# SBUF sums of a hybrid decoder layer: from GpSimd to VectorE, and the last norm's column sums ahead of its output products

## The chip, the cores and the metric

One core of one Trainium2 chip. The metric is the device time of one execution in microseconds (us), the median of three runs. The engines, as the profile names them: PE is TensorE (matmul), DVE is VectorE, ACT is ScalarE, POOL is GpSimd, SP is SyncE, which here issues all DMAs.

## The reference, cut to what matters

One decoder layer on 1024 tokens of width 1024, all in float32: an RMS norm and one input projection, split between dilated attention (8 heads) and an mLSTM (4 heads); an output projection; an MLP of width 4096; a gated embedding; a final norm.

```python
u = rms_norm(h, norm_mix_g); proj = u @ w_in
mix = concat([dilated_attention(q, k, v), mlstm(qc, kc, vm, i, f) * sigmoid(mo)])
h = h + mix @ w_out
u = rms_norm(h, norm_mlp_g)
h = h + square(relu(u @ w_up)) @ w_down
gate = sigmoid(rms_norm(h, norm_ple_g) @ w_ple_gate)
h = h + gate * (p @ w_ple)
return rms_norm(h, final_norm_g)
```

## The kernel before

Activations lie transposed: 128 features on the partitions, 1024 tokens along the free dimension, eight such tiles. Every float32 product is made of three fp32r matmuls (`mm3`, L101 to L103): an operand is split into a high part (ACT casts, L92) and a low part (DVE subtracts the high part, L93, or L85 in `load_w`), and high by high, high by low and low by high are summed in PSUM.

The stages, in the order of time:

- **Mixing** (to 560 us): the projections of q, k, v and the mLSTM's operands, the attention, the gates and the mLSTM heads. A tile scheduler that simulates the program chooses the order on each engine; projection matmuls stand between the attention's as filler. GpSimd does here the low parts of 24 weight tiles (`load_w(..., eng=G)`, L85), the rotation's product with the sines (`rope`, L339), two terms of the first norm's sum (L212), five sums on the gates' 32 rows (L263 to L278), the mask added to the decay rows `w` (`mlstm`, L594) and a sum of two blocks (L620).
- **Rest of the output projection and the operands** (560 to 660 us): the MLP's product is done by a scheme of seven block products in place of eight (`OPS`), so sums and differences of blocks are formed first: `operands` (L797) for the activations, `load_blocks` (L759 to L761, three sums to a weight block) for the weights, all on GpSimd.
- **Up-projection** (660 to some 970 us): 16 passes of `products`, two weight blocks each; `store` squares the result and writes it to DRAM (`zd`).
- **Down-projection** (some 970 to 1295 us): seven steps (`D_OPS`: b11, b21, t1, t2, b22, t3, t4) of eight groups `g`. Each group loads `y_r` and `wd_r` by DMA, splits both (L92, L93: `yh`/`yl`, `wdh`/`wdl`) and does 24 matmuls. Steps t1, t2, b22 and t3 need differences of weight blocks, which `weights` forms on GpSimd (L968, L975, L971). `wd_r` has four buffers, the split tiles three.
- **Gate, embedding and final norm** (1295 to 1395 us): `embed`, `gate`, then for four quarters of the output `final_cols(i)` (column sums on PE, a power on GpSimd, L1181) and `final(i)` (rows spread by PE, products on DVE, or on ACT and GpSimd, and the output's DMA). `ON_V[i]` lists the tiles whose product DVE does.

Each engine works through its own queue strictly in order, so an instruction that waits holds up all that stand behind it. GpSimd also has the powers (`pow`), and one-element copies (L1075) that make a DMA wait for a split.

Of the kernel before, what the change touches and what calls it, by code (L numbers as in the profile page):

```python
# [16 lines left out]
P = 128  # L17
# [28 lines left out]
def layer_kernel(ctx, tc, xT, wqk, wv, wvg, wmv, wmqk, wmo, wout, wup, wdown, wpg, wple, pT,  # L46
# [157 lines left out]
    for k in range(KT):  # L204
        if k:
            xr = unit("xr", F32)
            nc.sync.dma_start(xr, xT[k])
            X.append(split(pair("x"), xr, col[:, C_GMIX + k:C_GMIX + k + 1]))
        S.activation(xr, xr, AF.Square)
        eng = G if k in (1, 3) else V  # L210
        if eng in acc:
            eng.tensor_tensor(acc[eng], acc[eng], xr, op=ALU.add)  # L212
        else:
            acc[eng] = xr
        if k == 5:
            V.tensor_tensor(acc[V], acc[V], acc[G], op=ALU.add)
    col_sum(ssum, acc[V])
# [26 lines left out]
    def gates():  # L244
        g0, g1, g2, g3 = [unit("g", F32) for _ in range(4)]
        gb = col[:, C_GB:C_GB + 1]
        fr, t1, m, A, ir = g1[:R], g2[:R], g2[:R], g3[:R], g0[:R]
        wide = g3[:, :NB * 2 * R].rearrange("p (b g r) -> p b g r", b=NB, g=GC)
        S.copy(wide, gcol.unsqueeze(3).to_broadcast([P, NB, GC, NB]))
        for c in range(NCH):  # L250
            sl = slice(c * CH, (c + 1) * CH)
            ps = pmm.tile([P, CH], F32, name="g", tag="mm")
            for b in range(NB // 2):
                i = (c * NB // 2 + b) * 2 * R
                PE.transpose(ps[:2 * R, b * P:(b + 1) * P], g3[:, i:i + 2 * R], ident)
            S.activation(fr[:, sl], ps[R:2 * R], AF.Identity, bias=gb[R:2 * R])
            S.activation(ir[:, sl], ps[:R], AF.Identity, bias=gb[:R])
        V.scalar_tensor_tensor(t1, fr, -1.0, fr, op0=ALU.mult, op1=ALU.max)
        S.activation(t1, t1, AF.Exp, scale=-1.0)
        S.activation(t1, t1, AF.Ln, bias=1.0)  # L260
        V.scalar_tensor_tensor(fr, fr, 0.0, t1, op0=ALU.min, op1=ALU.subtract)
        V.tensor_tensor_scan(m, fr, ir, 0.0, op0=ALU.add, op1=ALU.max)
        G.tensor_tensor(ir, ir, m, op=ALU.subtract)  # L263
        G.tensor_tensor(fr[:, 1:], fr[:, 1:], m[:, :T - 1], op=ALU.add)
        G.tensor_tensor(fr, fr, m, op=ALU.subtract)
        mk = unit("mk", F32)[:R]
        nc.sync.dma_start(mk, maskT)
        G.tensor_tensor(fr, fr, mk, op=ALU.mult)
        V.tensor_tensor_scan(A, mk, fr, 0.0, op0=ALU.mult, op1=ALU.add)

        for j in range(T // 256):
            t0 = j * 256
            nc.sync.dma_start(arow[:, j, :256], A[2 * j::NB, t0:t0 + 256])
            nc.sync.dma_start(arow[:, j, 256:], A[2 * j + 1::NB, t0 + P:t0 + 256])
        nc.sync.dma_start(mk, lastT)
        end = sm.tile([R, 1], F32, name="end", bufs=1)
        V.tensor_tensor_reduce(mk, mk, A, 1.0, 0.0, op0=ALU.mult, op1=ALU.add, accum_out=end)
        G.tensor_tensor(ir, ir, A, op=ALU.subtract)  # L278
        return ir, m, end
# [19 lines left out]

    def values(src, evac, name, cw=256, eng=G):  # L300

# [32 lines left out]
    def rope(ps, sl):  # L334
        q = mp.tile([P, CH], F32, name="q")
        sh = mp.tile([P, CH], F32, name="sh")
        V.stream_shuffle(sh, ps, [i ^ 8 if i < 16 else i for i in range(32)])
        V.tensor_tensor(q, ps, cosS[:, sl], op=ALU.mult)
        G.tensor_tensor(sh, sh, sinS[:, sl], op=ALU.mult)  # L339
        V.tensor_tensor(q, q, sh, op=ALU.add)  # L340
        return q
# [4 lines left out]
    def project_qk(p, w=None):  # L346
# [22 lines left out]
        if w is None:  # L369
            proj(pmm, load_w(wqk[p], "wq", eng=G), X, ev_q, "q")  # L370
            proj(pmm, load_w(wqk[4 + p], "wk", eng=G), X, ev_k, "k")
            return QS, KD, kl
# [78 lines left out]
    def conv_silu(ct, stage, to=None):  # L451
# [4 lines left out]
        def ev(ps, c, sl):  # L456
# [14 lines left out]
            if to is None:  # L471
                nc.sync.dma_start(qkd[ct, :, sl], y)
        proj(pmm, load_w(wmqk[ct], "wm", eng=G), X, ev, "m")

    def out_gate(h, stage):

        def ev(ps, c, sl):
# [109 lines left out]
    def mlstm(h, c, ops, out):  # L587
# [5 lines left out]
        diag = w2.rearrange("p i (b s) -> p i b s", s=P)[:, :, 0::2]  # L593
        G.tensor_tensor(diag, diag, below.unsqueeze(1).unsqueeze(1).to_broadcast([P, 2, 2, P]), op=ALU.add)  # L594
        for i in range(2):
# [4 lines left out]
        for i in range(2):  # L600
# [15 lines left out]
            for b, at, n, t0 in blocks:  # L616
                bs = slice(b * P, (b + 1) * P)
                mm3(num[:, o + L - n:o + L], v[0][:, bs], v[1][:, bs], ph[:, at:at + n], pl[:, at:at + n],
                    j == 0 and at == 0, at > 0)
            G.tensor_tensor(w[:, P:L], w[:, P:L], w[:, L:], op=ALU.add)  # L620
            if j:
# [92 lines left out]
    with ExitStack() as tail:  # L714
# [38 lines left out]

        def load_blocks(src, name, raw=None, pool=None, eng=G):
            if raw is None:
                raw = wtc.tile([P, 8, L], F32, name=name + "_r", tag="wc", bufs=2)
            if src is not None:
                nc.sync.dma_start(raw[:, :4], src)
            eng.tensor_tensor(raw[:, 4:7:2], raw[:, 2:3].to_broadcast([P, 2, L]), raw[:, 1:4:2], op=ALU.subtract)  # L759
            eng.tensor_tensor(raw[:, 5], raw[:, 3], raw[:, 4], op=ALU.subtract)  # L760
            eng.tensor_tensor(raw[:, 7], raw[:, 0], raw[:, 5], op=ALU.subtract)  # L761
            wa = split(wtile(name, 3, "wa", pool), raw[:, 3:6])
# [25 lines left out]
        def operands(src, new, temp):  # L788
# [173 lines left out]
        def weights(key, g):  # L962
# [169 lines left out]
        def gate(k, sl, src, ga):  # L1132
# [82 lines left out]
        for o in range(1, NO - 1):  # L1215
# [92 lines left out]
```

## Time and profile before

| what | value |
|---|---|
| median of three runs | 1397.48 us (1396.22 to 1398.34) |
| the profiled execution's own time | 1397.32 us |
| its span, first to last instruction | 1395.5 us |
| PE busy | 1337.2 us, 96% of the span |
| DVE busy | 1018.9 us, 73% |
| ACT busy | 654.7 us, 47% |
| POOL busy | 408.2 us, 29% |
| mean granted TensorE clock | 0.984 of full speed |

All profile numbers come from one execution, the profiled one. An engine's busy time is the time in which one of its instructions ran; an instruction that was held up while it ran counts as busy for all of that time. Idle time of an engine that nobody waits for costs nothing.

### The profile page before, as it was taken

The numbers are of one execution on the slowest core, as the hardware profiler recorded it, in microseconds if no ns is written. First come the engines' busy times: TensorE is split into PE (matmuls) and PEld (weight loads), VectorE is DVE, ScalarE is ACT, GpSimd is POOL, SyncE is SP. The second block draws the span as 40 slices with busy tenths as digits, with TensorE's granted clock in tenths as the row PEclk, the third lists the DMA queues.
The fourth block names the chain that finished last, engine by engine and source line by source line (L and its number), as shares of the span: only waits on it lengthen the run. The fifth ranks groups of instructions, "written<-read, shape, count | busy, mean of one in ns | idle before, by whom it ended". The sixth has DMA issues, their size and how long they took to land.

```text
span 1395.5 us, 18439 instructions
## 1 busy us (share of the span) xinstructions
PE 1337.2 (96%) x6795; PEld 1121.1 (80%) x6795; DVE 1018.9 (73%) x1558; ACT 654.7 (47%) x1036; POOL 408.2 (29%) x271
## 2 busy tenths in 40 slices
PE   8999999999979999999999999999999899999995
PEld 6978988977868887787888888888887688888875
DVE  7788679589859796597566676567558965778896
ACT  6556545644446343256443334435334233465553
POOL 1432031142103222056333443332006771311012
PEclk9999999999999999999999999999999999999997
DMA  6111012222225347554164444446869674481323
GB/s 231 46 50 37 22 51 62 61 91 84 76 71 196 128 138 241 200 185 179 46 223 154 166 157 175 151 152 253 322 231 322 245 247 144 151 301 61 106 83 128
DMA packets 79017, 208.25 MB, mean 149 GB/s; under 512 B 7536, under 2 KB 19728, under 8 KB 74320
## 3 DMA queue, kind: packets, MB, share of 16 engines
q1 hardware_dynamic: 78928, 207.09, 43.1%
q8 instruction: 53, 0.87, 0.3%
q14 instruction: 36, 0.29, 0.1%
HBM read 146.74 MB, written 60.32 MB: 148 GB/s over the span
## 4 chain that ended last, share of the span: by engine, by line
PE 50%; DVE 11%; DMA 7%; issue 3%; POOL 2%; ACT 2%; SPq 0%; DVEq 0%; POOLq 0%; ACTq 0%
PE u L102 7%; PE u L103 7%; PE u L101 7%; PE d L102 6%; PE d L103 6%; PE d L101 6%; DMA wd_r<-wdown 2%; DMA w<-arow 1%; DMA wpg_r<-wpg 1%; POOL s L968 1%; DVE yl L93 1%; DMA in<-mixmd 1%; PE mo L101 1%; PE o L103 1%; PE mo L103 1%
## 5 line engine op out<-in xcount | busy, mean ns | idle before, releaser
L102 PE MATMUL u<-x,wuh 128*128 128x512 f32 x448 | 178.4, 398 | 0.2 <-DVE x L93 0.2
L101 PE MATMUL u<-x,wuh 128*128 128x512 f32 x448 | 176.0, 398 | 1.5 <-ACT x L92 1.5
L102 PE MATMUL d<-yl,wdh 128*128 128x512 f32 x432 | 169.0, 392 | 7.3 <-DVE yl L93 7.3
L103 PE MATMUL u<-x,wul 128*128 128x512 f32 x448 | 173.4, 398 | 0.0
L103 PE MATMUL d<-yh,wdl 128*128 128x512 f32 x432 | 168.3, 391 | 0.0
L101 PE MATMUL d<-yh,wdh 128*128 128x512 f32 x432 | 166.6, 391 | 0.0
L93 DVE TENSOR_TENSOR wul<-wu_r,wuh 128x768 fp32r<-128x768 f32 (+1 forms) x64 | 72.3, 1130 | 78.8 <-ACT wuh L92 78.8
L101 PEld LDWEIGHTS u<-x,wuh 128*128 128x128 f32 x448 | 84.9, 190 | 22.6 <-ACT x L92 2.4
L102 PEld LDWEIGHTS d<-yl,wdh 128*128 128x128 f32 x432 | 81.5, 189 | 25.9 <-DVE yl L93 8.9
L102 PEld LDWEIGHTS u<-x,wuh 128*128 128x128 f32 x448 | 85.0, 190 | 20.7 <-DVE x L93 0.5
L759 POOL TENSOR_TENSOR wu_r<-wu_r 128x512 f32<-128x512 f32 x32 | 47.0, 1468 | 186.3 <-DMA wu_r<-wup 161.2
L103 PEld LDWEIGHTS u<-x,wul 128*128 128x128 f32 x448 | 85.0, 190 | 20.1
L92 ACT CAST wuh<-wu_r 128x768 fp32r<-128x768 f32 (+1 forms) x64 | 60.5, 946 | 78.7 <-POOL wu_r L760 55.2
L103 PEld LDWEIGHTS d<-yh,wdl 128*128 128x128 f32 x432 | 81.6, 189 | 16.9
L101 PEld LDWEIGHTS d<-yh,wdh 128*128 128x128 f32 x432 | 81.4, 189 | 16.9
L93 DVE TENSOR_TENSOR yl<-y_r,yh 128x1024 fp32r<-128x1024 f32 x54 | 89.8, 1664 | 0.0
L93 DVE TENSOR_TENSOR wdl<-wd_r,wdh 128x1024 fp32r<-128x1024 f32 x30 | 42.5, 1416 | 51.3 <-ACT wdh L92 51.3
L412 ACT ACTIVATE pr<-pr,mn 128x128 f32<-128x128 f32 (+3 forms) x64 | 49.5, 774 | 56.0 <-PE av L415 30.4
L92 ACT CAST wdh<-wd_r 128x1024 fp32r<-128x1024 f32 x30 | 31.5, 1051 | 73.4 <-PE d L102 54.2
L92 ACT CAST wdh<-s 128x1024 fp32r<-128x1024 f32 x24 | 25.2, 1048 | 84.1 <-issue 70.5
L911 ACT COPY tmp<-u 128x512 f32<-128x512 f32 x48 | 28.0, 586 | 77.9 <-PE u L103 77.9
L93 DVE TENSOR_TENSOR wdl<-s,wdh 128x1024 fp32r<-128x1024 f32 x24 | 37.3, 1555 | 36.1 <-ACT wdh L92 36.1
(398 smaller groups left out, 3754.0 us busy)
## 6 DMA issues: line engine op xcount, KB each, us to landing
wd_r<-wdown SPq DMA_DIRECT2D x72, 512.0 KB
y_r<-zd SPq DMA_DIRECT2D x56, 512.0 KB
wu_r<-wup SPq DMA_DIRECT2D x32, 512.0 KB
zd<-zz SPq DMA_DIRECT2D x16, 1024.0 KB
zd<-zt SPq DMA_DIRECT2D x16, 1024.0 KB
wm_r<-wmqk SPq DMA_DIRECT2D x8, 512.0 KB
wo_r<-wout SPq DMA_DIRECT2D x16, 256.0 KB
hs<-h SPq DMA_DIRECT2D x8, 512.0 KB
```

Of the source, the lines that this page charges most:

```text
L92: S.copy(hi, src)
L93: V.tensor_tensor(lo, src, hi.bitcast(F32), op=ALU.subtract)
L101: PE.matmul(ps, wh, xh, start=start, stop=False, skip_group_check=more)
L102: PE.matmul(ps, wh, xl, start=False, stop=False, skip_group_check=more)
L103: PE.matmul(ps, wl, xh, start=False, stop=stop, skip_group_check=more)
L412: S.activation(pr[:, :nk], pr[:, :nk], AF.Exp, scale=-1.0, bias=mn[:, :1], accum_out=den)
L759: eng.tensor_tensor(raw[:, 4:7:2], raw[:, 2:3].to_broadcast([P, 2, L]), raw[:, 1:4:2], op=ALU.subtract)
L911: S.copy(tmp[key], ps)
L968: G.tensor_tensor(sw[g], a, b, op=ALU.subtract)
```

## The change

Every `tensor_tensor` sum, difference or product of SBUF tiles that GpSimd did goes to VectorE, but for the final products of the output and the powers. Since the scheduler simulates the program, the order on every engine is made anew. At the end, the column sums of all four quarters stand in the program ahead of the products of quarters 1 to 3, and `ON_V` gives DVE 6, 5 and 6 of the eight products of those quarters, where it had 6, 8 and 6.

```diff
-        eng = G if k in (1, 3) else V
+        eng = V
...
-        G.tensor_tensor(ir, ir, m, op=ALU.subtract)
-        G.tensor_tensor(fr[:, 1:], fr[:, 1:], m[:, :T - 1], op=ALU.add)
+        V.tensor_tensor(ir, ir, m, op=ALU.subtract)
+        V.tensor_tensor(fr[:, 1:], fr[:, 1:], m[:, :T - 1], op=ALU.add)
...
-    def values(src, evac, name, cw=256, eng=G):
+    def values(src, evac, name, cw=256, eng=V):
...
-        G.tensor_tensor(sh, sh, sinS[:, sl], op=ALU.mult)
+        V.tensor_tensor(sh, sh, sinS[:, sl], op=ALU.mult)
...
-            proj(pmm, load_w(wqk[p], "wq", eng=G), X, ev_q, "q")
+            proj(pmm, load_w(wqk[p], "wq", eng=V), X, ev_q, "q")
...
-        G.tensor_tensor(diag, diag, below.unsqueeze(1).unsqueeze(1).to_broadcast([P, 2, 2, P]), op=ALU.add)
+        V.tensor_tensor(diag, diag, below.unsqueeze(1).unsqueeze(1).to_broadcast([P, 2, 2, P]), op=ALU.add)
...
-            G.tensor_tensor(w[:, P:L], w[:, P:L], w[:, L:], op=ALU.add)
+            V.tensor_tensor(w[:, P:L], w[:, P:L], w[:, L:], op=ALU.add)
...
-        def load_blocks(src, name, raw=None, pool=None, eng=G):
+        def load_blocks(src, name, raw=None, pool=None):
...
-            eng.tensor_tensor(raw[:, 4:7:2], raw[:, 2:3].to_broadcast([P, 2, L]), raw[:, 1:4:2], op=ALU.subtract)
+            V.tensor_tensor(raw[:, 4:7:2], raw[:, 2:3].to_broadcast([P, 2, L]), raw[:, 1:4:2], op=ALU.subtract)
...
-                    G.tensor_tensor(ts[key][:, us], src[u][i0][:, s0], in1, op=o)
+                    V.tensor_tensor(ts[key][:, us], src[u][i0][:, s0], in1, op=o)
...
-                G.tensor_tensor(sw[g], a, b, op=ALU.subtract)
+                V.tensor_tensor(sw[g], a, b, op=ALU.subtract)
...
-                G.tensor_tensor(sw[g], a, sw[g], op=ALU.subtract)
+                V.tensor_tensor(sw[g], a, sw[g], op=ALU.subtract)
...
-                (G if c and k < 6 else V).tensor_tensor(fin[:, sl], fin[:, sl], ga, op=ALU.add)
+                V.tensor_tensor(fin[:, sl], fin[:, sl], ga, op=ALU.add)
...
-        ON_V = ((0, 1, 3, 4, 6), (0, 1, 3, 4, 5, 6), range(KT), (0, 2, 3, 5, 6, 7))
+        ON_V = ((0, 1, 3, 4, 6), (0, 1, 3, 4, 6, 7), (0, 1, 3, 4, 6), (0, 2, 3, 5, 6, 7))
...
-                                   "t3": [lambda: final_cols(1)], "t4": [lambda: final(1), lambda: final_cols(2)]})
-        final(2)
+                                   "t3": [lambda: final_cols(1)], "t4": [lambda: final_cols(2)]})
         final_cols(3)
-        final(3)
+        for i in range(1, 4):
+            final(i)
```

In the changed program the lines lie two further up from L263 on (four in the last loop but one place). Three places show what the new order does.

**Step t1 of the down-projection.** GpSimd before: `h<-yl` is the one-element copy, `s<-wd_r` a difference for t1, `s<-wd_r,s` one for t2.

```order
L968 TENSOR_TENSOR s<-wd_r 128x1024 x2
L1075 COPY h<-yl 1x1
L975 TENSOR_TENSOR s<-wd_r,s 128x1024 x2
L1075 COPY h<-yl 1x1
L975 TENSOR_TENSOR s<-wd_r,s 128x1024 x2
```

VectorE in the changed program, at the same place; before, its queue held there only the splits `wdl` and `yl`.

```order
L966 TENSOR_TENSOR s<-wd_r 128x1024
L93 TENSOR_TENSOR wdl<-s,wdh 128x1024
L996 TENSOR_TENSOR state<-state,sq 128x512
L93 TENSOR_TENSOR yl<-y_r,yh 128x1024
L973 TENSOR_TENSOR s<-wd_r,s 128x1024
L93 TENSOR_TENSOR wdl<-s,wdh 128x1024
L93 TENSOR_TENSOR yl<-y_r,yh 128x1024
L973 TENSOR_TENSOR s<-wd_r,s 128x1024 x3
L93 TENSOR_TENSOR wdl<-s,wdh 128x1024
```

The differences, each of which waits for its DMA, now stand between the splits that PE waits for.

**The end, VectorE before:** `out` is a final product (`bp_12113`, `bp_12140` and `bp_12165` are the spread rows of quarters 1, 2 and 3), `ra` the step between a quarter's column sums and its power, `h` and `state` the last gate and row sum.

```order
L1195 SCALAR_TENSOR_TENSOR out<-h,col,bp_12113 128x256 x6
L1137 SCALAR_TENSOR_TENSOR ga<-ga,e 128x256
L1138 SCALAR_TENSOR_TENSOR h<-ga,h 128x256
L1180 SCALAR_TENSOR_TENSOR ra_12136<-cs_12131,seps 128x2
L1138 SCALAR_TENSOR_TENSOR h<-ga,h 128x256
L1146 TENSOR_TENSOR state<-state,ga 128x256
L1195 SCALAR_TENSOR_TENSOR out<-h,col,bp_12140 128x256 x8
L1180 SCALAR_TENSOR_TENSOR ra_12161<-cs_12156,seps 128x2
L1195 SCALAR_TENSOR_TENSOR out<-h,col,bp_12165 128x256 x6
```

VectorE in the changed program (`bp_12131`, `bp_12149`, `bp_12168` for quarters 1, 2, 3):

```order
L1136 SCALAR_TENSOR_TENSOR h<-ga,h 128x256
L1144 TENSOR_TENSOR state<-state,ga 128x256
L1178 SCALAR_TENSOR_TENSOR ra_12118<-cs_12113,seps 128x2
L1193 SCALAR_TENSOR_TENSOR out<-h,col,bp_12131 128x256 x5
L1178 SCALAR_TENSOR_TENSOR ra_12127<-cs_12122,seps 128x2
L1193 SCALAR_TENSOR_TENSOR out<-h,col,bp_12131 128x256
L1193 SCALAR_TENSOR_TENSOR out<-h,col,bp_12149 128x256 x5
L1193 SCALAR_TENSOR_TENSOR out<-h,col,bp_12168 128x256 x6
```

The last gate steps come before the products of quarter 1, and the last `ra` before those of quarter 2. GpSimd's queue there is now:

```order
L1179 TENSOR_TENSOR rb_12119<-ra_12118,mhalf 128x2
L1196 TENSOR_TENSOR out<-out,rows 128x256 x5
L1179 TENSOR_TENSOR rb_12128<-ra_12127,mhalf 128x2
L1196 TENSOR_TENSOR out<-out,rows 128x256 x2
```

Before, the powers of quarters 2 and 3 followed each other; now five products of quarters 1 and 2 stand between them.

**End of the attention, PE before:** `mvp` is the last projection filler, `s`, `tp` and `av` are the attention's scores, transposes and value products.

```order
L103 MATMUL mvp<-mv_h,x 128x256
L405 MATMUL s<-kd,qs 128x512
L406 MATMUL s<-kl_120,qs 128x512
L405 MATMUL s<-kd,qs 128x256
L406 MATMUL s<-kl_120,qs 128x256
L422 MATMUL tp<-ident,pr 128x128 x3
```

PE in the changed program:

```order
L103 MATMUL mvp<-mv_h,x 128x256
L429 MATMUL av<-ph,vv 128x256
L430 MATMUL av<-pl,vv 128x256
L429 MATMUL av<-ph,vv 128x128
L430 MATMUL av<-pl,vv 128x128
L420 MATMUL tp<-ident,pr 128x128 x8
L413 MATMUL av<-ident,den 128x128 x2
```

From the last filler to the next projection matmul stand 95 matmuls before and 139 in the changed program: the filler is used up earlier.

## Rows read from the trace of the kernel before

**Rows 1.** The page, part 1: busy us (share of the span) xinstructions

```profile
PE 1337.2 (96%) x6795; PEld 1121.1 (80%) x6795; DVE 1018.9 (73%) x1558; ACT 654.7 (47%) x1036; POOL 408.2 (29%) x271
```

**Rows 2.** Stretches of 50 us: PE, PEld, DVE, ACT, POOL busy (x), PEclk, DMA share, GB/s

```profile
300.00:350.00 50.00, 48.66 (x260) 39.70 (x259) 47.70 (x94) 19.98 (x49) 12.80 (x5) 1.00 0.28 95
...
600.00:650.00 50.00, 49.54 (x213) 39.64 (x212) 45.05 (x40) 31.70 (x40) 32.64 (x19) 1.00 0.54 189
...
1050.00:1100.00 50.00, 44.19 (x191) 35.25 (x189) 46.51 (x25) 22.07 (x26) 36.97 (x17) 1.00 0.81 285
```

**Rows 3.** Waits: who waited for whom: us in total, times, longest us

```profile
PE d L102 <- DVE yl L93: 7.3, 4, 3.5
...
PE bp L130 <- POOL rb L1181: 6.8, 3, 3.2
...
POOL w L594 <- DMA w<-arow: 62.1, 6, 40.3
```

**Rows 4.** Timeline, GpSimd and VectorE, step t1: start us, us, engine line op

```profile
1079.33 4.74 POOL L975 TENSOR_TENSOR s<-wd_r,s 128x1024 f32<-128x1024 f32 x2
...
1079.25 5.90 DVE L93 TENSOR_TENSOR yl<-y_r,yh 128x1024 fp32r<-128x1024 f32 x1
```

**Rows 5.** Groups of VectorE by shape: count | busy us, mean ns | idle before

```profile
L93 DVE TENSOR_TENSOR yl<-y_r,yh 128x1024 fp32r<-128x1024 f32 x54 | 89.8, 1664 | 0.0
...
L93 DVE TENSOR_TENSOR y<-y_r,y 128x1024 fp32r<-128x1024 f32 x2 | 2.4, 1216 | 0.6 <-ACT y L92 0.6
...
L759 DVE TENSOR_TENSOR wpg_r<-wpg_r 128x512 f32<-128x512 f32 x8 | 5.5, 689 | 4.8 <-DMA wpg_r<-wpg 4.8
...
L760 DVE TENSOR_TENSOR wpg_r<-wpg_r 128x256 f32<-128x256 f32 x8 | 3.3, 417 | 0.0
...
L93 DVE TENSOR_TENSOR wdl<-wd_r,wdh 128x1024 fp32r<-128x1024 f32 x30 | 42.5, 1416 | 51.3 <-ACT wdh L92 51.3
...
L93 DVE TENSOR_TENSOR wdl<-s,wdh 128x1024 fp32r<-128x1024 f32 x24 | 37.3, 1555 | 36.1 <-ACT wdh L92 36.1
```

**Rows 6.** Five stretches about the places of the change, columns as in group 2

```profile
60.00:387.50 327.50, 318.59 (x1937) 277.89 (x1937) 261.63 (x594) 173.93 (x361) 76.78 (x37) 1.00 0.19 59
...
387.50:408.80 21.30, 15.79 (x97) 12.40 (x95) 14.64 (x42) 10.28 (x22) 0.00 (x0) 0.92 0.05 13
...
425.00:560.00 135.00, 131.19 (x785) 114.55 (x784) 106.20 (x228) 57.81 (x116) 35.61 (x33) 0.97 0.52 171
...
650.00:668.00 18.00, 16.24 (x57) 12.83 (x56) 11.32 (x14) 10.85 (x18) 9.39 (x9) 0.72 0.40 147
...
1057.00:1112.00 55.00, 47.75 (x200) 38.03 (x199) 53.66 (x29) 20.73 (x24) 40.20 (x19) 0.97 0.80 289
```

**Rows 7.** Timeline of the operands, GpSimd and ScalarE, before the up-projection

```profile
644.06 2.00 POOL L759 TENSOR_TENSOR wu_r<-wu_r 128x512 f32<-128x512 f32 x1 [5.64 <-DMA wu_r<-wup]
...
651.75 1.28 POOL L797 TENSOR_TENSOR t<-h,t 128x512 f32<-128x512 f32 x1
...
653.07 1.14 ACT L92 CAST x<-h 128x512 fp32r<-128x512 f32 x2 [2.39 <-POOL t L797]
```

**Rows 8.** Timeline of one pass of the up-projection

```profile
809.83 1.43 POOL L759 TENSOR_TENSOR wu_r<-wu_r 128x512 f32<-128x512 f32 x1 [0.27 <-DMA wu_r<-wup]
...
814.78 1.07 DVE L93 TENSOR_TENSOR wul<-wu_r,wuh 128x768 fp32r<-128x768 f32 x1 [0.35 <-ACT wuh L92]
...
823.35 0.57 ACT L913 COPY zz<-u 128x512 f32<-128x512 f32 x1
```

**Rows 9.** Timeline of the end, VectorE and GpSimd

```profile
1378.62 2.42 DVE L1195 SCALAR_TENSOR_TENSOR out<-h,col,bp 128x256 f32<-128x256 f32 x6
...
1383.98 3.22 DVE L1195 SCALAR_TENSOR_TENSOR out<-h,col,bp 128x256 f32<-128x256 f32 x8 [0.96 <-ACT rows L1189]
...
1387.12 0.15 DVE L1180 SCALAR_TENSOR_TENSOR ra<-cs,seps 128x2 f32<-128x2 f32 x1
...
1389.32 1.41 POOL L1198 TENSOR_TENSOR out<-out,rows 128x256 f32<-128x256 f32 x2 [1.28 <-ACT rows L1189]
```

More of the change, by code (lines that the diff above doesn't have):

```diff
@@ L214, in layer_kernel @@
             acc[eng] = xr
-        if k == 5:
-            V.tensor_tensor(acc[V], acc[V], acc[G], op=ALU.add)
     col_sum(ssum, acc[V])
@@ L262, in gates @@
         V.tensor_tensor_scan(m, fr, ir, 0.0, op0=ALU.add, op1=ALU.max)
-        G.tensor_tensor(ir, ir, m, op=ALU.subtract)
-        G.tensor_tensor(fr[:, 1:], fr[:, 1:], m[:, :T - 1], op=ALU.add)
-        G.tensor_tensor(fr, fr, m, op=ALU.subtract)
+        V.tensor_tensor(ir, ir, m, op=ALU.subtract)
+        V.tensor_tensor(fr[:, 1:], fr[:, 1:], m[:, :T - 1], op=ALU.add)
+        V.tensor_tensor(fr, fr, m, op=ALU.subtract)
         mk = unit("mk", F32)[:R]
         nc.sync.dma_start(mk, maskT)
-        G.tensor_tensor(fr, fr, mk, op=ALU.mult)
+        V.tensor_tensor(fr, fr, mk, op=ALU.mult)
         V.tensor_tensor_scan(A, mk, fr, 0.0, op0=ALU.mult, op1=ALU.add)
@@ L277, in gates @@
         V.tensor_tensor_reduce(mk, mk, A, 1.0, 0.0, op0=ALU.mult, op1=ALU.add, accum_out=end)
-        G.tensor_tensor(ir, ir, A, op=ALU.subtract)
+        V.tensor_tensor(ir, ir, A, op=ALU.subtract)
         return ir, m, end
@@ L369, in project_qk @@
         if w is None:
-            proj(pmm, load_w(wqk[p], "wq", eng=G), X, ev_q, "q")
-            proj(pmm, load_w(wqk[4 + p], "wk", eng=G), X, ev_k, "k")
+            proj(pmm, load_w(wqk[p], "wq", eng=V), X, ev_q, "q")
+            proj(pmm, load_w(wqk[4 + p], "wk", eng=V), X, ev_k, "k")
             return QS, KD, kl
@@ L472, in ev @@
                 nc.sync.dma_start(qkd[ct, :, sl], y)
-        proj(pmm, load_w(wmqk[ct], "wm", eng=G), X, ev, "m")
+        proj(pmm, load_w(wmqk[ct], "wm", eng=V), X, ev, "m")
     def out_gate(h, stage):
@@ L482, in ev @@
             nc.sync.dma_start(sgd[h, :, sl], sg)
-        proj(pmm, load_w(wmo[h], "wo", eng=G), X, ev, "mo")
+        proj(pmm, load_w(wmo[h], "wo", eng=V), X, ev, "mo")
     def stage(name):
@@ L758, in load_blocks @@
                 nc.sync.dma_start(raw[:, :4], src)
-            eng.tensor_tensor(raw[:, 4:7:2], raw[:, 2:3].to_broadcast([P, 2, L]), raw[:, 1:4:2], op=ALU.subtract)
-            eng.tensor_tensor(raw[:, 5], raw[:, 3], raw[:, 4], op=ALU.subtract)
-            eng.tensor_tensor(raw[:, 7], raw[:, 0], raw[:, 5], op=ALU.subtract)
+            V.tensor_tensor(raw[:, 4:7:2], raw[:, 2:3].to_broadcast([P, 2, L]), raw[:, 1:4:2], op=ALU.subtract)
+            V.tensor_tensor(raw[:, 5], raw[:, 3], raw[:, 4], op=ALU.subtract)
+            V.tensor_tensor(raw[:, 7], raw[:, 0], raw[:, 5], op=ALU.subtract)
             wa = split(wtile(name, 3, "wa", pool), raw[:, 3:6])
@@ L967, in weights @@
                 a, b = wraw(g, A21), wraw(g, A22)
-                G.tensor_tensor(sw[g], a, b, op=ALU.subtract)
+                V.tensor_tensor(sw[g], a, b, op=ALU.subtract)
             elif key == "t3":
                 a, b = wraw(g, A21), wraw(g, A11)
-                G.tensor_tensor(a, a, b, op=ALU.subtract)
+                V.tensor_tensor(a, a, b, op=ALU.subtract)
                 return a
@@ L1120, in fetch @@
                         G.tensor_copy(raw[:1, 0, :1], X[i]["t4"][1].bitcast(F32)[:1, :1])
-                wblocks[o].append(load_blocks(src, "wpg", raw, (wt0, wt1)[i], V))
+                wblocks[o].append(load_blocks(src, "wpg", raw, (wt0, wt1)[i]))
         def fetch_emb(o):
```

## The prediction

> **What bounds the kernel now.** I read the busy times of the whole span first. PE is busy 96% of it, DVE 73%, POOL 29% [rows 1]. So the change can win no more than PE's idle time and the time in which PE ran at a lowered clock, and VectorE has room on the average. Averages hide stages, so next come the stretches of 50 us [rows 2]: PE idles 5.8 us of 1050 to 1100, where DVE is busy 46.5 of 50 and POOL 37.0; at 300 to 350 and 600 to 650 DVE is busy 47.7 and 45.0. Third, the waits of PE by who released it [rows 3]: the two longest entries are 7.3 us for `yl`, a low part that VectorE makes, and 6.8 us for `rb`, the power that GpSimd makes at the end. Fourth, what VectorE does when PE waits for `yl` [rows 4]: a `yl` that starts at 1079.25 runs for 5.90 us, and over the same time GpSimd forms two differences `s` in 4.74 us, 2.37 each. A subtraction of that size alone takes 1.216 us on VectorE [rows 5]. The two engines hold each other up while both work on SBUF; each `s` on VectorE would have cost 1.22.
>
> **What the move costs VectorE.** Durations are DVE's own rows for the same size [rows 5]: 1.216 us for 128x1024, 0.689 for 128x512, 0.417 for 128x256.
>
> - sums of the up-projection's weights: 32 blocks x (0.689 + 0.417 + 0.417) = 48.7 us
> - differences of the down-projection's weights: 32 x 1.216 = 38.9
> - low parts in the mixing stage: 24 x 1.216 = 29.2
> - rotation 16 x 0.689 = 11.0, operands 16 x 0.689 = 11.0, mask 8 x 0.689 = 5.5, row sums 5 x 0.689 = 3.4, two-block sums 16 x 0.417 = 6.7 at most
> - gates and first norm: 6 x 1.216 = 7.3
>
> Together 162 us. Against it stands the stretch that goes. In the down-projection it can be counted: `yl` 54 x (1.664 - 1.216) = 24.2, `wdl` 30 x (1.416 - 1.216) = 6.0 and 24 x (1.555 - 1.216) = 8.1, together 38.3 us [rows 5], as much as the 38.9 that comes in. I take the same balance for the other stages, so DVE stays near 1020 us busy; were the mixing stage's part (29.2 + 11.0 + 5.5 + 6.7 + 7.3) not balanced, near 1080. So the moved work as such costs the end nothing. What cover that leaves: were there no balance, the down-projection's 39 us would lie beside a PE that is busy to 100% in most of its stretches.
>
> **Terms, each at the place where PE idles now.**
>
> (a) Step t1, 1057 to 1112: PE busy 47.75 of 55, and its granted clock is 0.97 of the full 2.4 GHz [rows 6]. Idle 7.25, and 0.03 x 55 = 1.65 for the clock: 8.9 us is all there is. In the new order each `s` stands in VectorE's queue between the splits, at 1.2 us instead of behind a `yl` of 5.9. The transfers are the same as before; what is late next is their landing, with DMA 0.80 busy in this stretch, which should be about where PE then wants them. I take -8.5, bounds -8.9 and 0.
>
> (b) Start of the up-projection, 650 to 668: PE busy 16.24 of 18 at a clock of 0.72 [rows 6], so 1.8 idle and 5.0 for the clock. The activation's operands `t` are formed on GpSimd behind weight sums, the first of which waited 5.64 us for its DMA, and ACT's casts waited 2.39 for `t` [rows 7]. On VectorE the sums are short, but the casts and the column sums stay, and the same DMA can hold VectorE. At worst those 2.39 stay and come on top, +2.4; at best all 6.8 go. I take -2, nearer to nothing, since the clock falls after gaps that the casts leave as well.
>
> (c) The end. The last gate steps and a row sum no longer wait behind six products (2.42 us), nor `ra` of the last quarter behind eight (3.22) [rows 9], and VectorE has three products fewer (3 x 0.403 = 1.2). The last power, though, now has five products of GpSimd ahead of it, 5 x 0.705 = 3.5 us [rows 9]. At best 3.2 + 1.2 = 4.4 is won; at worst the 3.5 falls whole on the last quarter and only the 1.2 is won, +2.3. I take -1.5, between them.
>
> (d) End of the attention, 387.5 to 408.8: 21.3 us with PE busy 15.79 at a clock of 0.92 [rows 6], so 5.5 + 1.7 = 7.2 us lost on 95 matmuls without filler. The new order leaves 139 there. At the same loss for each, 44 x 7.2/95 = +3.3; I take +3, bounds 0 and +7 (twice the rate).
>
> (e) The rest of the mixing stage, 60 to 387.5: PE idles 8.9 us in all [rows 6], spread over many short waits. The shorter low parts may win some, VectorE's longer queue may lose some: I take -1, and half of the idle time, 4.5, as bounds on either side.
>
> Nothing for three stages. mLSTM heads, 425 to 560: idle 3.8 of 135 [rows 6]. Up-projection: in one pass the last weights start their sum when the DMA has landed at 809.8, the low part starts at 814.8 and takes 1.07, and the next pass begins about 823.3, where `zz` is copied [rows 8]; 7.4 us of slack hide 1.5 us of sums. Gate stage: its five row sums, 3.4 us, against stretch that goes.
>
> Sum: -8.5 - 2 - 1.5 + 3 - 1 = -10. The profiled execution took 1397.32 us (span 1395.5 and 1.8 around it), 0.2 under the median, so I forecast 1387.3, **1387**.
>
> **Rivals.**
>
> *The DMA takes the place of GpSimd at t1.* VectorE now holds its splits while a difference waits for its weight block, and PE waits for the splits. Then (a) shrinks to nothing: 1397.3 - 1.5 = 1396 with the other terms, 1395 if a little stays. For it: DMA is 81% busy there, 285 GB/s [rows 2]. Against it: the longest waits are for a `yl` in which VectorE worked, not stood. It decides from 7 us of waits on.
>
> *The mask waits for its DMA in VectorE's queue (slower).* In the mLSTM heads the mask is added to `w` on GpSimd, which waited for that DMA 62.1 us in six times, one of them 40.3 [rows 3]. On VectorE such a wait holds the low parts behind it. The other five waits make 62.1 - 40.3 = 21.8 us; if all fell on work that PE wants, with (a) won, 1387 + 22 = 1409. It decides from 10 us on, when the gain is gone. Against it: GpSimd was early there, with little else to do, and VectorE with 106 us of 135 busy [rows 6] comes to the same place later.
>
> *VectorE becomes the bound (slower).* If no stretch goes back, each us of POOL turns into 1.216/2.37 = 0.51 of DVE. The three fullest stretches [rows 2] become 47.7 + 6.5 = 54.2, 45.0 + 16.6 = 61.7 and 46.5 + 18.9 = 65.4 of 50 us: 31 us over, 1428. Against it stand the 38.3 us of stretch that rows 5 show. The Trainium skill has the rule in "Perfetto Trace Analysis", section "Optimizing Scalar/DVE Operations": with a saturated DVE it can make sense to hand work to ScalarE or even GPSIMD, so this change would go the wrong way; the same section adds that those two share a read port, so that moving work between them might not help. By the first half the time would be 1428; the 5.90 us of rows 4 bear out the second half.
>
> *More is won:* (b) and (c) at their best, (a) as taken: -8.5 - 6.8 - 4.4 + 3 - 1 = -18, 1379.
>
> **Numbers.** A measurement of this kernel tells 0.2%, 2.8 us, from no change. My forecast, 1380 to 1394, gets 0.70; the DMA at t1 0.12, half of it faster and half within 2.8 us; the mask 0.09 (0.07 slower, 0.02 the same); the bound on VectorE 0.04, slower; the larger gain, 1370 to 1380, 0.05. Faster 0.70 + 0.06 + 0.05 = 0.81, the same 0.08, slower 0.11. The range 1378 to 1398 leaves out most of the last rival, of the mask and of the bound.
>
> **What would show it.** Right: `yl` near 1.22 us on the mean, DVE at 1020 to 1080 busy, no wait of PE for `yl` between 1050 and 1110, longer gaps than 7 us at the end of the attention, and a shorter stretch from the last gate product to the end. Wrong: VectorE standing for `wd_r` at t1 or for `arow` in the heads with PE waiting behind it, or DVE above 1100 us. If t1 keeps its 7 us of idle time, step (a) has failed and with it most of the forecast.

## The result, and the profile after

| | before | changed |
|---|---|---|
| median | 1397.91 us (1396.22 to 1400.28) | 1384.59 us (1381.49 to 1385.74) |
| ratio | | 0.990, 95% interval 0.9878 to 0.9922 |
| profiled execution: time, span | 1397.32, 1395.5 | 1385.74, 1383.9 |

Faster by 13.3 us; 1387 had been forecast, with 1378 to 1398 as the range. The two profiled executions differ by 11.6 us of span. Where these lie is read off PE's timeline, by the first matmul of each stage:

| stage | before | changed | difference | forecast |
|---|---|---|---|---|
| start to the first `u` (mixing, output projection, operands) | 650.4 | 647.8 | -2.5 | +2 (terms d, e) |
| up-projection, to the first `d` | 322.8 | 316.7 | -6.1 | -2 (b) |
| down-projection, to the first `pg` | 316.2 | 313.5 | -2.7 | -8.5 (a) |
| gate, embedding, norm, to the end of the span | 106.2 | 105.9 | -0.3 | -1.5 (c) |

The sum was near in part by luck, since errors of its terms cancelled: (a) gave 5.8 us and (c) 1.2 less than forecast, the mixing stage 4.5 and (b) 4.1 more. First the busy times of the whole span, part 1 of the page, for the changed kernel:

```profile
PE 1330.2 (96%) x6795; PEld 1120.7 (81%) x6795; DVE 1021.7 (74%) x1774; ACT 655.6 (47%) x1039; POOL 58.0 (4%) x55
```

GpSimd gave up 350 us of busy time, and VectorE, which took over 216 instructions (estimated at 162 us), is busy 1021.7 us where it was 1018.9 [rows 1]. Its groups by line and shape tell why (columns as in [rows 5]):

```profile
L93 DVE TENSOR_TENSOR yl<-y_r,yh 128x1024 fp32r<-128x1024 f32 x54 | 65.6, 1216 | 0.0
L93 DVE TENSOR_TENSOR wdl<-wd_r,wdh 128x1024 fp32r<-128x1024 f32 x30 | 36.6, 1220 | 43.8 <-ACT wdh L92 43.8
L93 DVE TENSOR_TENSOR wdl<-s,wdh 128x1024 fp32r<-128x1024 f32 x24 | 29.3, 1219 | 20.2 <-ACT wdh L92 20.2
...
L757 DVE TENSOR_TENSOR wu_r<-wu_r 128x512 f32<-128x512 f32 x32 | 22.1, 692 | 23.8 <-DMA wu_r<-wup 23.3
L973 DVE TENSOR_TENSOR s<-wd_r,s 128x1024 f32<-128x1024 f32 x16 | 19.3, 1217 | 5.4 <-DMA wd_r<-wdown 5.4
```

All three splits take 1.22 us now, where they took 1.66, 1.42 and 1.56, and the moved sums cost what was reckoned for them. Of the three fullest stretches (columns as in [rows 2]) the first and the third are less full for VectorE than they were and the second is 2.3 us fuller, and PE has lost nearly all of its idle time in the third:

```profile
300.00:350.00 50.00, 49.77 (x276) 41.77 (x275) 47.03 (x102) 23.47 (x54) 0.00 (x0) 1.00 0.29 91
...
600.00:650.00 50.00, 50.00 (x217) 40.54 (x216) 47.30 (x63) 36.23 (x48) 0.00 (x0) 1.00 0.60 210
...
1050.00:1100.00 50.00, 49.60 (x220) 40.76 (x218) 42.93 (x43) 22.82 (x26) 9.88 (x4) 1.00 0.85 313
```

Next, stretches that answer to those of [rows 6], moved with their stage: end of the attention (from the last filler to the next, all 139 matmuls), start of the up-projection, start of the down-projection (which had no idle time before), step t1.

```profile
377.36:405.52 28.16, 22.17 (x139) 17.58 (x138) 19.90 (x58) 15.11 (x33) 0.00 (x0) 0.94 0.05 13
647.50:665.50 18.00, 18.00 (x87) 14.67 (x86) 14.81 (x23) 11.66 (x18) 2.22 (x2) 1.00 0.28 105
964.50:1019.50 55.00, 51.25 (x214) 41.83 (x213) 29.44 (x29) 20.30 (x20) 2.63 (x5) 0.94 0.77 264
1048.40:1103.40 55.00, 54.60 (x242) 44.90 (x240) 46.97 (x47) 24.96 (x29) 9.88 (x4) 1.00 0.86 315
```

The second and the fourth are full, at full clock: 6.8 and 8.5 us of idle time and half clock are gone. The third is new: 3.75 us of idle time, and a clock of 0.94, worth 0.06 x 55 = 3.3 us. So some 7 us of what t1 gave are given back ahead of it. Cut by the matmuls themselves (each of the seven steps has 192 into `d`; most steps take 43.5 us in both kernels), t1 reads, before and then changed:

```profile
1060.19:1113.80 53.61, 46.36 (x193) 36.90 (x192) 52.27 (x28) 20.09 (x23) 39.67 (x18) 0.97 0.80 287
...
1058.85:1102.49 43.64, 43.64 (x192) 36.13 (x193) 38.24 (x39) 20.97 (x25) 9.88 (x4) 1.00 0.83 304
```

So t1 gave 10.0 us, while the first step, b11, went from 43.5 to 50.3 and b21 from 43.5 to 44.1. The waits of PE name the engines (columns as in [rows 3]):

```profile
PE o L101 <- DVE t L664: 5.1, 1, 5.1
...
PE d L101 <- ACT wdh L92: 3.7, 1, 3.7
PE bp L130 <- POOL rb L1179: 3.3, 1, 3.3
...
PE cs L1173 <- DVE state L1144: 2.7, 2, 1.6
PE pg L101 <- DVE ga L1157: 2.3, 2, 1.8
```

No wait for `yl` is left. The one for `wdh`, ScalarE's cast, is the new one. ScalarE's timeline there (start us, duration us; the bracket holds the idle time before it and what ended it):

```profile
980.84 1.05 ACT L92 CAST wdh<-wd_r 128x1024 fp32r<-128x1024 f32 x1 [9.18 <-PE d L102]
981.80 1.05 ACT L92 CAST yh<-y_r 128x1024 fp32r<-128x1024 f32 x1
986.28 1.04 ACT L92 CAST wdh<-wd_r 128x1024 fp32r<-128x1024 f32 x1 [3.44 <-PE d L102]
987.24 1.99 ACT L92 CAST yh<-y_r 128x1024 fp32r<-128x1024 f32 x2
989.13 1.04 ACT L92 CAST wdh<-wd_r 128x1024 fp32r<-128x1024 f32 x1
```

and PE's:

```profile
990.22 2.08 PE L101 MATMUL d<-yh,wdh 128*128 128x512 f32 x4 [3.75 <-ACT wdh L92]
...
993.80 0.63 PE L103 MATMUL d<-yh,wdl 128*128 128x512 f32 x1
```

The cast at 986.28 waits until PE has finished a group, since it needs a tile that this group still read. PE then wants the last cast, at 989.13, which stands three casts behind in the queue. PE resumes at 990.22, and its matmuls are 0.63 us long in the trace where at full clock they are 0.39. The two orders of ScalarE's queue at this place, from the last square `zz` on:

```
before:   zz, wdh, yh x2, wdh x2, yh, wdh, ...
changed:  zz, wdh, yh, wdh, yh x2, wdh x2, ...
```

Before, the second pair (`yh`, `wdh`) stood ahead of the `wdh` that waits for PE; now that one is ahead of the pair. No line of the diff touches these casts; the simulating scheduler put them so.

### The profile page after: what moved, and what is told of

It is laid out like the page before. It is cut to its first block, busy times and chain, and to the rows that moved or that the text cites. A ratio compares the mean times of both kernels' runs of the same rounds, so it can differ in the third digit from the quotient of the medians.

```text
span 1383.9 us, 18363 instructions
## 1 busy us (share of the span) xinstructions
PE 1330.2 (96%) x6795; PEld 1120.7 (81%) x6795; DVE 1021.7 (74%) x1774; ACT 655.6 (47%) x1039; POOL 58.0 (4%) x55
## 5 line engine op out<-in xcount | busy, mean ns | idle before, releaser
L93 DVE TENSOR_TENSOR wul<-wu_r,wuh 128x768 fp32r<-128x768 f32 (+1 forms) x64 | 69.6, 1087 | 65.2 <-ACT wuh L92 65.2
L93 DVE TENSOR_TENSOR wdl<-wd_r,wdh 128x1024 fp32r<-128x1024 f32 x30 | 36.6, 1220 | 43.8 <-ACT wdh L92 43.8
L93 DVE TENSOR_TENSOR yl<-y_r,yh 128x1024 fp32r<-128x1024 f32 x54 | 65.6, 1216 | 0.0
L405 DVE CUSTOM_DVE_ANT_0 pr<-s,biasS 128x512 f32<-128x512 f32 (+2 forms) x96 | 51.0, 551 | 12.3 <-PE tp L420 7.2
L92 ACT CAST yh<-y_r 128x1024 fp32r<-128x1024 f32 x54 | 56.5, 1047 | 7.1 <-DMA y_r<-zd 7.1
L93 DVE TENSOR_TENSOR pl<-tp,ph 128x512 fp32r<-128x512 f32 (+1 forms) x80 | 49.7, 631 | 10.7 <-ACT ph L92 6.3
```

The source lines that it names most:

```text
L92: S.copy(hi, src)
L93: V.tensor_tensor(lo, src, hi.bitcast(F32), op=ALU.subtract)
L405: V.tensor_tensor_reduce(pr[:, ks], s[:, :n], biasS[:, b0 + o:b0 + o + n], 1.0, -2 * LOW, op0=ALU.add, op1=ALU.min, accum_out=mn[:, o // C ...
```

## The experiments

**One part of the change at a time, in the kernel before** (e1 to e4; the kernel before, run beside them, has a median of 1396.21 us).

```diff
 # e1, in weights(), all three forms
-                G.tensor_tensor(sw[g], a, b, op=ALU.subtract)
+                V.tensor_tensor(sw[g], a, b, op=ALU.subtract)
 # e2, in load_blocks (three sums) and operands
-        def load_blocks(src, name, raw=None, pool=None, eng=G):
+        def load_blocks(src, name, raw=None, pool=None, eng=V):
-                    G.tensor_tensor(ts[key][:, us], src[u][i0][:, s0], in1, op=o)
+                    V.tensor_tensor(ts[key][:, us], src[u][i0][:, s0], in1, op=o)
```

e3 has every hunk of the diff up to L620 of the kernel before, e4 those of the row sums, `ON_V` and the order of `final_cols` and `final`.

> The kernel before with one part of the change: the 32 differences of the down-projection's weight blocks on VectorE. My theory, gains belong to their places: the four waits of PE for yl in step t1 (7.3 us) and the half clock after them go, the mean of yl falls from 1.66 us to about 1.25, and the time falls by 7 to 9 us, to some 1389; the first 18 us of the up-projection keep their 1.8 us of idle time and their clock of 0.72. Rival, the DMA takes GpSimd's place: PE's idle time in t1 stays near 7 us, now with VectorE standing for wd_r, and the time stays within 3 us of 1397.

e1 took 1388.41 us, ratio 0.9939 (0.9917 to 0.9962). Two of its stretches, the start of the up-projection and t1:

```profile
650.90:668.90 18.00, 15.47 (x59) 10.68 (x58) 11.22 (x14) 11.54 (x20) 9.23 (x9) 0.83 0.39 147
1057.30:1112.30 55.00, 53.66 (x236) 43.81 (x235) 48.27 (x50) 23.82 (x28) 9.87 (x4) 1.00 0.84 307
```

The stretch of t1 has 1.3 us of idle time left of 7.25, at full clock, and `yl` is at 1.22 us on the mean; the first 18 us of the up-projection keep their gaps and a low clock. From the first `d` to the first `pg` it is 308.0 us, 8.2 less than before. The DMA did not take GpSimd's place.

> The kernel before with one part of the change: the sums of the weight blocks (load_blocks) and the operands of the up-projection on VectorE. My theory: PE's gaps and the half clock in the first 18 us of the up-projection go (6.4 us won), but ScalarE's queue at the start of the down-projection gets the order of the changed kernel, in which two casts that wait for PE stand ahead of the pair of casts that PE wants, which costs a gap of some 3.7 us and 3.5 us of half clock: net -1 to +2 us, 1396 to 1399, with the waits in t1 as before. Rival: the gap in the down-projection comes from the DMA being late after the faster up-projection or from the other parts; then it is absent or small here and the time is 1390 to 1392.

e2 took 1393.48 us, ratio 0.9986 (0.9966 to 1.0007): no change that can be told. The start of the up-projection, of the down-projection, and t1:

```profile
646.60:664.60 18.00, 18.00 (x87) 14.63 (x86) 14.91 (x23) 11.68 (x18) 2.22 (x2) 1.00 0.30 104
963.30:1018.30 55.00, 51.25 (x214) 41.81 (x213) 29.44 (x29) 20.17 (x20) 2.63 (x5) 0.94 0.76 263
1057.30:1112.30 55.00, 49.91 (x213) 40.61 (x212) 49.12 (x28) 22.12 (x25) 46.00 (x18) 0.97 0.78 278
```

The up-projection is 6.4 us shorter (first `u` to first `d` 316.4), and the new gap is there to the hundredth, 3.75 us with a clock of 0.94. So both belong to this part. The waits in t1 shrank to 5.1 us in two, and the whole step t1 takes 50.6 us, 3.0 less than before, so that the down-projection lost 3.7 us in all, not 7; that is why the time came out lower than the first theory had it.

> The kernel before with one part of the change: the mixing stage's sums, low parts, rotation, mask and gates on VectorE. My theory: only the mixing stage moves, its end comes 2.5 us earlier, the time falls by 2 to 4 us to 1394, and the later stages keep their waits. Rival: VectorE's longer queue with the mask's DMA wait in it loses in the heads what the attention wins, and without the other parts the gain is nothing or a loss: 1397 to 1402.

e3 took 1396.12 us, ratio 1.0002 (0.9983 to 1.0020). Its largest waits of PE:

```profile
PE d L102 <- DVE yl L93: 7.3, 4, 3.5
PE o L101 <- DVE t L664: 7.0, 1, 7.0
```

The attention ends 4.1 us earlier than before (its last scores at 387.6, where they were at 391.7), but 2 us of that are lost again at the output projection, where PE waits 7.0 us in one piece for a sum that frees a PSUM tile; before, such waits were 2.4 us long. My figure of 2 to 4 us was too high; the rival was the better one in size, though not in its mechanism (below, the mask).

> The kernel before with one part of the change: the last norm's column sums ahead of the products of quarters 1 to 3, ON_V, and the row sums on VectorE. My theory from the two profiles, in which the stretch from the first gate matmul to the end is 106.2 us before and 105.9 after: within 1 us of nothing, 1397. Rival, my forecast's term: -1.5 us or more.

e4 took 1396.71 us, ratio 1.0003 (0.9988 to 1.0019). The end is worth nothing, as the theory had it.

**What makes the new gap.** f1 returns the six sums of the last of 16 passes to GpSimd, whereby the scheduler's order of the casts is that of the kernel before again; f2 to f4 ran beside it (kernel before, beside them, 1395.12 us).

```diff
-            products([load_blocks(wup[f, i], "wu") for i in range(2)], X, ev, "u", own)
+            products([load_blocks(wup[f, i], "wu", eng=G if f == 15 else V) for i in range(2)], X, ev, "u", own)
```

> The changed kernel, with the six weight sums of the last up-projection pass alone back on GpSimd. In its order ScalarE's queue at the start of the down-projection again has the pair of casts that PE wants next ahead of the cast that waits for PE, as before. My theory, the order of ScalarE's queue makes the new gap: the 3.75 us gap some 25 us into the down-projection and the half clock behind it go, everything else stays, and the time is 6 to 7 us under the changed kernel's, 1377 to 1379. Rival, the weight's DMA (or the store of zt, whose memory the third split pair reuses) lands late because the up-projection ends earlier: the gap stays within 1 us of 3.7 and the time within 2 us of 1385.

> The changed kernel once more, beside the three above. Its gap of 3.75 us some 25 us into the down-projection comes from the order of a queue and so comes again, to 0.1 us; a gap from DMA that lands early or late would differ by more. The time is 1384 to 1386.

f1 took 1379.80 us, ratio 0.9893 (0.9878 to 0.9907); f4, the changed kernel again, 1385.64 us, ratio 0.9934 (0.9918 to 0.9951), with the gap at 3.75 us once more. f1's start of the down-projection and t1:

```profile
964.60:1019.60 55.00, 55.00 (x244) 45.51 (x243) 31.80 (x31) 22.52 (x23) 2.87 (x6) 1.00 0.82 291
1048.40:1103.40 55.00, 53.68 (x238) 44.14 (x237) 50.84 (x53) 23.97 (x28) 12.98 (x5) 1.00 0.87 317
```

and its ScalarE there:

```profile
980.93 1.05 ACT L92 CAST wdh<-wd_r 128x1024 fp32r<-128x1024 f32 x1 [9.67 <-PE d L102]
981.89 2.00 ACT L92 CAST yh<-y_r 128x1024 fp32r<-128x1024 f32 x2
984.20 1.05 ACT L92 CAST wdh<-wd_r 128x1024 fp32r<-128x1024 f32 x1 [0.31 <-DMA zd<-zt]
986.38 1.05 ACT L92 CAST wdh<-wd_r 128x1024 fp32r<-128x1024 f32 x1 [1.12 <-PE d L102]
```

The second pair is cast by 985.25, ahead of the cast that waits for PE, and PE never stops. f1's first `d` is at 964.6 where the changed kernel's is at 964.5, so the up-projection ended no earlier or later, and the store of `zt`, whose memory that pair reuses, held it by 0.31 us only: it was the order. The gain is 4.8 us against the first median of the changed kernel and 5.8 against f4, which ran beside it, a little under the 6 to 7 expected; 1.3 us of a new wait in the second stretch, for a VectorE sum, make up part of it.

**Do the engines hold each other up, or was GpSimd only slow?** f2 is the changed kernel, in which GpSimd also forms differences that nobody reads. It adds 32 subtractions on GpSimd, two for each group of t1 and t2 (shown for t1; the tile `dum` and its memset are left out here).

```diff
+        def dummy(a):
+            for c in range(2):
+                G.tensor_tensor(dum, a[:, c * CH:(c + 1) * CH], dum, op=ALU.subtract)
...
                 V.tensor_tensor(sw[g], a, b, op=ALU.subtract)
+                dummy(a)
```

> The changed kernel, and beside it GpSimd subtracts in steps t1 and t2 that nobody reads: for each group two of 128x512 elements of the same wd_r (as many elements as the differences that it made in the kernel before), into a tile of their own. My theory, the two engines hold each other up on SBUF: yl and wdl in t1 and t2 stretch to 2 to 6 us again, VectorE gets nearly full there, and PE waits 5 to 9 us for VectorE's results in t1, 1390 to 1394 in all. Rival, GpSimd was only slow, and PE waited since the difference came late from it: work on GpSimd that nobody waits for changes nothing, yl stays at 1.22 us, and the time is within 2 us of the changed kernel's.

f2 took 1397.51 us, ratio 1.0012 (0.9996 to 1.0028): the whole gain is gone, and the time is above the 1390 to 1394 expected. That is 12 us above f4, and 18 above f1, which like f2 has no gap at the start of the down-projection. PE's largest wait is for `yl` again:

```profile
PE d L102 <- DVE yl L93: 10.7, 5, 5.4
```

VectorE's timeline in t1, two stretches of it:

```profile
1075.43 1.21 DVE L93 TENSOR_TENSOR wdl<-s,wdh 128x1024 fp32r<-128x1024 f32 x1
1076.57 1.21 DVE L93 TENSOR_TENSOR yl<-y_r,yh 128x1024 fp32r<-128x1024 f32 x1
1077.70 3.48 DVE L978 TENSOR_TENSOR s<-wd_r,s 128x1024 f32<-128x1024 f32 x3
...
1089.70 1.48 DVE L978 TENSOR_TENSOR s<-wd_r,s 128x1024 f32<-128x1024 f32 x1 [6.25 <-DMA wd_r<-wdown]
1091.10 2.42 DVE L93 TENSOR_TENSOR wdl<-s,wdh 128x1024 fp32r<-128x1024 f32 x1
1093.44 2.29 DVE L93 TENSOR_TENSOR yl<-y_r,yh 128x1024 fp32r<-128x1024 f32 x1
```

and GpSimd's over the same time:

```profile
1070.32 17.03 POOL L962 TENSOR_TENSOR dum<-wd_r,dum 128x512 f32<-128x512 f32 x3 [2.43 <-DMA wd_r<-wdown]
...
1091.18 9.26 POOL L962 TENSOR_TENSOR dum<-wd_r,dum 128x512 f32<-128x512 f32 x5
```

No VectorE instruction reads `dum`, and yet from 1091 on `wdl` and `yl` take 2.3 to 2.4 us in place of 1.21. That can't be a late result of GpSimd's; it is the other engine's work on SBUF. The size is not all stretch, though: from 1070 to 1087 GpSimd's three halves took 5.7 us each while VectorE ran at 1.21, and since these read `wd_r`, they kept its buffers, so the next block landed late: VectorE stood 6.25 us for that DMA. This side of the experiment I had not expected, and its two parts are not separated. The Trainium skill, "SBUF — State Buffer", section "Who interferes with whom", has DVE and GpSimd share one pair of ports under an exclusive lock, over which a DVE instruction with two SBUF inputs contends with a GpSimd instruction that reads SBUF. Both stretches agree with that, 5.7 us for GpSimd's halves in the one and 2.3 us for VectorE's splits in the other.

**What the other parts are worth in the best version.** g1 is f1 once more; g2 has the mixing stage on GpSimd as before, g3 two edits of it, g4 the old end; f3 is the changed kernel with the old end (g1 to g4 beside a kernel before of 1398.42 us, f3 beside that of f1, 1395.12).

```diff
 # g3, in f1's kernel
-        V.tensor_tensor(diag, diag, below.unsqueeze(1).unsqueeze(1).to_broadcast([P, 2, 2, P]), op=ALU.add)
+        G.tensor_tensor(diag, diag, below.unsqueeze(1).unsqueeze(1).to_broadcast([P, 2, 2, P]), op=ALU.add)
-            V.tensor_tensor(w[:, P:L], w[:, P:L], w[:, L:], op=ALU.add)
+            G.tensor_tensor(w[:, P:L], w[:, P:L], w[:, L:], op=ALU.add)
```

g2 is the kernel before with e1, e2 and e4 and f1's edit. f3 and g4 undo e4's hunks.

> The changed kernel with the weight sums of the last up-projection pass on GpSimd, once more, beside the three below: 1378 to 1381, and no gap of PE before a cast in the first 40 us of the down-projection.

> As the first, with the whole mixing stage on GpSimd as before. My theory, the move in the mixing stage is worth nothing: it wins 3 to 4 us up to the end of the attention and loses as much again at the output projection, where PE now waits 5 to 8 us for a sum that frees a PSUM tile, so the time is within 2 us of the first, and that gap is back to 1 to 3 us, as in the kernel before. Rival, the stage's move counts in full: 3 us or more above the first.

> As the first, with the mask's addition to w and the sum of two blocks in the mLSTM heads back on GpSimd. My theory: the loss at the output projection comes from the order in which SP's queue issues the loads of t, not from VectorE's wait for w (4.0 us in the profile of the changed kernel), so the time follows the gap that the new order leaves there, between 1375 and 1381. Rival of the prediction, the mask's DMA wait in VectorE's queue costs PE time: then taking it out wins 3 us or more in the heads, between the first upd and the last fb.

> As the first, with the end of the kernel before. My theory: the end is worth nothing, within 1 us of the first, PE's two gaps of 3 us for rb back and the stretch behind the last of them shorter by as much. Rival, the forecast's term: 1.5 us or more above the first.

> The changed kernel with the end of the kernel before: the products of quarter 1 ahead of the column sums of quarters 2 and 3, ON_V as before, row sums on GpSimd. My theory, the end is worth nothing: within 1 us of the changed kernel, 1384 to 1386; PE's two gaps for rb of 3 us are back, and the stretch from the last column sums to the end is 1 to 2 us shorter. Rival, my forecast's term of -1.5: 1386.5 or more.

| run | median us (lowest to highest) | ratio to before, interval |
|---|---|---|
| g1 | 1379.31 (1375.38 to 1381.53) | 0.9859 (0.9841 to 0.9878) |
| g2, mixing on GpSimd | 1378.92 (1378.60 to 1382.95) | 0.9870 (0.9854 to 0.9886) |
| g3, mask and block sums on GpSimd | 1382.32 (1379.89 to 1384.12) | 0.9886 (0.9872 to 0.9901) |
| g4, old end | 1379.19 (1379.03 to 1379.71) | 0.9865 (0.9849 to 0.9880) |
| f3, changed kernel, old end | 1384.64 (1380.63 to 1387.94) | 0.9927 (0.9902 to 0.9952) |

The mixing stage's move and the end's are worth nothing that can be measured. In g2 the wait at the output projection is small again, 2.3 us in two.

With the mixing stage on VectorE (the changed kernel, e3, f1 to f4, g1, g4) the longest of these waits is 4.9 to 7.8 us, without it (before, e1, e2, e4, g2) 1.1 to 2.8. g3 missed its expectation of 1375 to 1381: its median is 3.0 to 3.4 us above the three others, with two waits of 3.8 us together there and one of 3.3 us for a sum into `h` (L660), and taking the mask away from VectorE won nothing. The measure that the expectation named, first `upd` to last `fb`, is 141.9 us against g1's 152.2, but only since the last `fb` stands earlier in the new order: from the first `upd` to the first `u` it is 237.2 us against 235.1. In g4 PE's waits for `rb` are back, and cost nothing:

```profile
PE bp L130 <- POOL rb L1179: 7.2, 3, 3.5
```

So f1's version (g1) takes 1379.3 to 1379.8 us, some 5 to 6 us under the changed kernel, and g2 and g4 can't be told from it. They show that the gain needs neither the move in the mixing stage nor the new end; leaving out both at once was not tried.

## Why the prediction was right, point by point

**What bounds the kernel, and the price on VectorE.** Right. The 162 us went in and nearly as much stretch came out: +2.8 us of DVE in all. In the down-projection `yl` and `wdl` lost 38.1 us against [rows 5], and the moved differences take 38.9. The balance "for the other stages", which I had only taken over from the down-projection, held.

**(a) Step t1, -8.5: right at its place, wrong for its stage.** At its place it measured -10.0. "8.9 us is all there is" was too low: of the 10.1 us by which t1 was longer than an undisturbed step, 7.25 were idle time and 2.8 slower matmuls, where 1.65 had been reckoned for the clock. e1 gives -8.2 us for the stage. In the changed kernel it is -2.7. The step that failed is "what is late next is their landing": what was late next was a cast, some 70 us ahead of t1, in a queue that the diff does not touch, and its reorder was brought by (b)'s part (e2). The working followed the new order on VectorE, GpSimd and PE; ScalarE's, where this stands, had no place in it. f1, without it, gives 307.7 us for the stage, -8.5, and g1 306.3, -9.9.

**(b) Start of the up-projection, -2: mis-sized; it measured -6.1, in e2 -6.4.** The bound of -6.8 held. I chose a value near nothing, "since the clock falls after gaps that the casts leave as well". With the sums on VectorE the casts left no gap at all, and the half clock (5 of the 6.8 us) went with the 1.8 us of gaps: the stretch from 647.5 to 665.5 shows 18.00 us busy at 1.00. Here the lowered clock and the gaps ahead of it went as one loss, in the changed kernel and in e2.

**(c) The end, -1.5: nothing** (e4, f3, g4). The loss that I had named as a bound came in part. The end of the changed kernel, VectorE:

```profile
1372.60 0.15 DVE L1178 SCALAR_TENSOR_TENSOR ra<-cs,seps 128x2 f32<-128x2 f32 x1
```

then GpSimd:

```profile
1372.34 2.09 POOL L1196 TENSOR_TENSOR out<-out,rows 128x256 f32<-128x256 f32 x3 [0.24 <-POOL out L1196]
1374.39 0.70 POOL L1179 TENSOR_TENSOR rb<-ra,mhalf 128x2 f32<-128x2 f32 x1
```

The last `ra` is ready at 1372.75; the power starts at 1374.39, behind three of the five products. PE's single remaining wait for `rb`, 3.3 us, stands in the waits above; the two others (6.8 us in three before [rows 3]) are gone, but the products that filled them come after the last row of `bp` now: from that to the end of the span it is 8.5 us, where it was 7.1. The working also left out PE's longer waits for `state` and `ga` in the list above (2.7 and 2.3 us; before, `cs` and `pg` waited 1.0 us each for `ga`), and the clock. The whole stage, before and then changed:

```profile
1289.30:1395.50 106.20, 87.62 (x473) 74.11 (x471) 87.29 (x160) 49.94 (x93) 18.16 (x19) 0.93 0.32 104
...
1278.00:1383.90 105.90, 88.83 (x473) 75.22 (x471) 84.20 (x162) 51.00 (x96) 11.73 (x17) 0.91 0.33 105
```

PE idles 1.5 us less, but the same 473 matmuls take 1.2 us longer at the lower clock.

**(d), (e) Mixing, +2: -2.5 in the profile, nothing in the median** (e3, g2). At the last `av` of the attention, the 2345th matmul on record in both kernels, 3.2 us are won. (d) was right in that the stretch without filler grew, from 387.51 to 408.76 before to 377.36 to 405.52, but mis-sized: by the measure of (d) it loses 6.0 + 1.7 = 7.7 us where it lost 7.2, so +0.5 and not +3. "At the same loss for each" failed; the first 45 of the 139 matmuls are done in 6.9 us at full clock with 1.0 us idle. (e) was right in sign and mis-sized: from 60 us to the last filler PE idles 5.9 us, where it idled 8.9, so -3.0 and not -1. The heads and the output projection, set to nothing, gave back 0.7 together.

**Rivals.** The DMA at t1: refuted by e1 and by the fourth stretch of after. VectorE as the bound: DVE went from 73% to 74% ("those two" in the prediction's sentence on it are DVE and GPSIMD). The mask: g3 won nothing by taking it back, and VectorE's wait for it was short (the waits of the changed kernel):

```profile
DVE w L592 <- DMA w<-arow: 4.0, 4, 2.0
```

Still open: why PE waits longer at the output projection with the mixing stage on VectorE. The trace shows VectorE's `t` waiting for the DMA of `t`, issued late from SP's queue; that was not tried by itself.

## What to carry to other kernels

Price a move from GpSimd to VectorE by the stretch that goes as well as by the work that comes: `yl` at 1.66 us on the mean against 1.22 alone was the largest part of the answer here. Where a scheduler makes the order, read the new order of every engine that the bounding engine waits for, also where no line was touched: one cast in the wrong place cost 5 to 6 us of the 15 to 19 that were to be had (f1 and g1, each against the kernel before beside it). Where a lowered clock follows gaps, as at the start of the up-projection, ask first whether the gaps go altogether; not every gap has one behind it (1.3 us of idle time in the stretch of t1 in e1 and in f1, at a clock of 1.00).

## What the runs showed of the hardware

Which engine stands still changes: in f2 the same pair of engines ran first with GpSimd at 5.7 us for 128x512 elements and VectorE undisturbed, then with VectorE's splits at 2.3 us and GpSimd's halves at 1.9 (9.26 us for five). And the one that stands still can wait out several instructions of the other. In e2 a difference of GpSimd's takes 9.53 us, beside six subtractions that VectorE does in a row at 1.21 each, and ends 2.3 us after the last of them; right behind it VectorE's `wdl` takes 5.80 us, beside two differences of GpSimd's in 4.75:

```profile
1070.28 9.53 POOL L968 TENSOR_TENSOR s<-wd_r 128x1024 f32<-128x1024 f32 x1 [2.08 <-DMA wd_r<-wdown]
1079.89 4.75 POOL L975 TENSOR_TENSOR s<-wd_r,s 128x1024 f32<-128x1024 f32 x2
...
1079.92 5.80 DVE L93 TENSOR_TENSOR wdl<-s,wdh 128x1024 fp32r<-128x1024 f32 x1 [2.38 <-ACT wdh L92]
```

GpSimd's copies of one element, 0.57 us each on the mean before, take 1.26 in the changed kernel. The mean hides the spread: in f1 one of them takes 9.06 us, from 1077.53 on, while VectorE's instructions follow each other without a pause, and it ends at 1086.59, when VectorE stands idle for 0.40 us. No wait of PE names these copies.
